# Where a kernel prepares its mixed weight blocks: two of twenty-six moved from the output projection to the up projection, and the weights' high parts taken one chunk earlier in the output projection

## The chip, the cores and the metric

The kernel runs on one core of a Trainium2 chip. The metric is device time in microseconds (us) of one execution; lower is better. Each kernel is run several times and the median counts. One more execution is taken with the hardware profiler; it has a time of its own.

## What is computed

A decoder layer for 256 tokens of width 2048 in float32: RMS norm, one input projection, eight attention heads beside a causal pooling mixer, an output projection into the residual stream, and a gated MLP with a causal convolution of width 3. Cut to what the change touches:

```python
x = x + jnp.concatenate([a, m], axis=-1) @ w_out
h = rms_norm(x, ffn_norm_g)
u = h @ w_up                                  # 2048 -> 2 * 5632
y = conv_b + sum(conv_w[i] * u_pad[:, i:i + S] for i in range(3))
gate, val = jnp.split(y, 2, axis=-1)
x = x + (jax.nn.silu(gate) * val) @ w_down    # 5632 -> 2048
```

## The kernel before

**Chunks.** All weights stream once from HBM in chunks of 128 x 2048 floats (1 MB), in the order of use, numbered c. A chunk feeds two steps of TensorE (PE). The output projection is chunks 32 to 48, the first third of the up projection is chunks 49 to 80. An output-projection block is two chunks (four steps) and yields 256 of the 2048 features; there are eight, 0 to 7. An up-projection group is four chunks: a gate block and a value block. The MLP runs in three thirds of 8, 8 and 6 groups; each third's up projection is followed by its share of the down projection.

**High and low parts.** To get float32 accuracy from float32r matmuls, each raw chunk (`raw`) is split: ACT copies it to a rounded high part (`wh`, line 158 or 181), and VectorE (DVE) subtracts to get the low part (`wl`, line 159 or 187). PE multiplies high by high and low (one 512-column matmul, line 263) and low by high (one 256-column matmul, line 265); these two I call a pair. There are four `wh` buffers, three `wl` buffers and five `raw` buffers (four, and one opened in the output projection); a raw buffer is free again when its low part is made.

**When a chunk is split.** `layer` records the instructions of all engines in one pass over the steps, and each engine executes its own in that order. When chunk c-2 is about to be used, chunk c is handled. Below chunk 52 (`FROM`) both parts of chunk c are recorded there (`split`). From 52 on only the low part of c is (`low`), and the high part of c+1 (`high`), so that ACT is three chunks ahead of PE and DVE two:

```python
            if c < FROM:
                split(c)
            if FROM - 1 <= c < len(rows) - 1:
                high(c + 1)
            if FROM <= c < len(rows):
                splits.append(lambda c=c: low(c))
```

**Mixed blocks.** The down projection saves an eighth of the products of some chunks with sums of weight blocks (Winograd's form of Strassen's seven products). Those sums are made on the chip: `make` loads a 1 MB block (`in_mix`, through the SP queue as all loads), does three DVE operations on it (lines 195, 196, 197), and writes it back to HBM through the POOL queue (`mixed`, line 198); the down projection loads it later like a chunk. The raw buffer of a mix block is free when that write has landed. There are 26 makes. `MAKES` names the chunks of the output projection at which the first ones stand, `PAIRS` the places in each third's up projection, in units of four chunks.

**The end of an output block.** When PE has finished a block, `residual` runs: an ACT copy and a DVE add of the two accumulator halves (`fs`, lines 532 and 533), which frees the accumulator; the DVE add to the residual (`x2f`, line 707); an ACT square and a DVE add into the running sum of squares (`xs`, line 712, and line 713). One step later `x2_split` makes the activations of the next stage (`x2h`, ACT line 721, DVE line 723). After block 7, `sums2` (lines 772 and 745 to 752) reduces the sum of squares, and two small POOL DMAs (`row_d`, `row`, lines 754 and 756) turn it into a row on all partitions, from which `stats2` (lines 384 to 391) makes the norm's factors `rrow`. The first gate block needs them when it leaves its accumulator (line 533 and, times `rrow`, line 788, `u`). Two accumulators exist, so the third up block cannot start before the first has left.

Of the kernel before, what the change touches and what calls it, by code (L numbers as in the profile page):

```python
# [42 lines left out]
CH = 2048  # L43
HALF = CH // 2
AHEAD = 5
FROM = 52
AFTER_DOWN = (97, 145)
RAWS = 4

# [3 lines left out]
WOFF = ((32, 32), (16, 36))  # L53
THIRDS = ((0, 8), (8, 16), (16, 22))
SEVEN = ((1, 2, 3, 4, 5), (1, 2, 3, 4, 5), (1, 2, 3))
MAKES = (40, 42, 44, 46, 48, 50)
PAIRS = ((2, 3, 4, 5, 6, 7), (0, 1, 2, 3, 4, 5, 6, 7), (0, 1, 2, 3, 4, 5))
SOFF, SPAD = 32, 64


# [6 lines left out]
def plan():  # L67

    rows, makes = [(k, i) for i, k in enumerate(24 * ["tok"] + 25 * ["feat"])], list(MAKES)
    n = t = 0  # L70
    for (g0, g1), sevens, pairs in zip(THIRDS, SEVEN, PAIRS):
        makes += [len(rows) + 4 * p + 3 for p in pairs]
        c = rows[-1][1] + 1
        rows += [("feat", c + i) for i in range(4 * (g1 - g0))]
        c = rows[-1][1] + 1
        for i in range(2 * (g1 - g0)):
            if i % (g1 - g0) in sevens:
                rows.append(("sum", t))
                t += 1
            rows.append(("rest" if i % (g1 - g0) in sevens else "tok", c + i))  # L80
    assert len(makes) == t, (len(makes), t)
    return rows, makes
# [12 lines left out]
def layer(ctx: ExitStack, tc: tile.TileContext, xT, wts, mix, par, rel_d, ident_d, icnt_d, out):  # L95
# [24 lines left out]

    raws, wparts = {}, {}
    rows, makes = plan()
    mixed = [dram.tile([P, CH], F32, name=f"mixed{i}", tag=f"mixed{i}") for i in range(len(makes))]
    order = [r for c in range(len(rows)) for r in [c] + [("make", i) for i, m in enumerate(makes) if m == c]]
# [49 lines left out]
    def split(c):  # L174
        split_piece(c, 0, CH)
        release(c)

    def high(c):

        wparts[c] = w, = (high_tile(c)[:, :width(c)],)  # L180
        nc.scalar.activation(w, raws[c][:, :width(c)], AF.Copy)  # L181

    def low(c):

        wh, = wparts[c]
        wl = low_tile(c)[:, :width(c)]
        nc.vector.tensor_tensor(wl, raws[c][:, :width(c)], wh.bitcast(F32), op=OP.subtract)  # L187
        wparts[c] = wh, wl
        release(c)
# [788 lines left out]
    for u in range(n):  # L978
# [4 lines left out]
        elif u in starts:  # L983
            c, now[0] = starts[u] + 2, u
# [6 lines that stand above are left out]
# [91 lines left out]
```

## Time and profile before

| | us |
|---|---|
| median of 3 runs (1008.5 to 1010.6) | 1008.98 |
| the profiled execution's own time | 1016.39 |
| its span, first to last instruction | 1014.6 |
| PE busy | 999.8 |
| PE weight loads busy | 858.5 |
| DVE busy | 846.1 |
| ACT busy | 540.2 |
| POOL busy | 75.0 |
| mean granted TensorE clock | 0.993 |
| moved by DMA | 285.34 MB, 281 GB/s |

The span is the stretch that the profile covers; the own time has a little around it. An engine's busy time is the sum over its instructions, and matmul ends are modelled, so that PE's idle time is better read from the list of its waits. In the trace's rows the first number is the start, the second the duration, both in us; in brackets stands the idle time of the engine before the instruction and what ended it. "L263" is line 263.

### The profile page before, as it was taken

How to read it: one execution, taken by the hardware profiler on the slowest of the kernel's cores; microseconds unless marked ns; L12 is line 12 of the kernel's file. 1: busy time of each engine (PE TensorE's matmuls, PEld its weight loads, DVE VectorE, ACT ScalarE, POOL GpSimd, SP SyncE). 2: the span in 40 equal slices, each digit the busy share in tenths (PEclk: the TensorE clock that was granted, in tenths of full speed). 3: DMA queues.
4: the chain of work that ended last, by engine and by line, in shares of the span. 5: the costliest groups of instructions: out<-in, count | busy, mean ns of one | idle time of the engine just before them, and what ended most of it. 6: DMA issues, size and time to landing. Idle time of an engine off the chain costs nothing.

```text
span 1014.6 us, 13410 instructions
## 1 busy us (share of the span) xinstructions
PE 999.8 (99%) x5276; PEld 858.5 (85%) x5276; DVE 846.1 (83%) x960; ACT 540.2 (53%) x543; POOL 75.0 (7%) x145
## 2 busy tenths in 40 slices
PE   9999999999988999999999999999999999999998
PEld 8888888888877888888888888888888888888886
DVE  6776858858886999899888879999998887899986
ACT  6554545555444554555646455454665745555642
POOL 0202232200002500000000000000000000000000
PEclk9999999999998999999999999999999999999999
DMA  9958785687888987777779777777787977777782
GB/s 348 320 207 271 258 260 177 218 291 290 302 321 284 308 287 283 292 257 289 294 287 379 267 293 278 264 276 278 281 307 314 385 262 301 276 273 277 288 321 85
DMA packets 47679, 285.34 MB, mean 281 GB/s; under 512 B 6568, under 2 KB 9000, under 8 KB 18176
## 3 DMA queue, kind: packets, MB, share of 16 engines
q1 hardware_dynamic: 39184, 245.29, 66.7%
q0 software_dynamic: 8432, 39.20, 10.6%
q8 instruction: 41, 0.67, 0.2%
q14 instruction: 22, 0.18, 0.1%
HBM read 248.94 MB, written 35.52 MB: 280 GB/s over the span
## 4 chain that ended last, share of the span: by engine, by line
PE 71%; DVE 14%; issue 6%; DMA 5%; ACT 2%; POOL 1%; SPq 0%; DVEq 0%; POOLq 0%; ACTq 0%
PE ps_feat L263 29%; PE ps_down L849 21%; PE ps_feat L265 15%; DVE wl L187 5%; PE ps_val L241 4%; PE ps_tok L251 2%; DVE y L800 1%; DVE fs L533 1%; DVE y L798 1%; DMA raw<-in_mix 1%; DVE raw L195 1%; ACT wh L181 1%; DVE u L788 1%; DVE wl L159 1%; DMA qT<-q1d 1%
## 5 line engine op out<-in xcount | busy, mean ns | idle before, releaser
L263 PE MATMUL ps_feat<-x2h,wh 128*128 128x512 f32 x1406 | 490.3, 395 | 5.1 <-DVE x2h L723 3.5
L265 PE MATMUL ps_feat<-x2h,wl 128*128 128x256 f32 x1408 | 392.9, 279 | 2.6 <-DVE wl L187 2.4
L187 DVE TENSOR_TENSOR wl<-raw,wh 128x2048 fp32r<-128x2048 f32 (+1 forms) x155 | 339.2, 2195 | 18.7 <-PE ps_down L849 7.1
L181 ACT ACTIVATE wh<-raw 128x2048 fp32r<-128x2048 f32 (+1 forms) x155 | 285.3, 1844 | 79.0 <-PE ps_down L849 57.2
L263 PEld LDWEIGHTS ps_feat<-x2h,wh 128*128 128x128 f32 x1406 | 266.1, 189 | 65.8 <-DVE x2h L723 3.8
L265 PEld LDWEIGHTS ps_feat<-x2h,wl 128*128 128x128 f32 x1408 | 266.8, 189 | 3.5 <-DVE wl L187 3.0
L159 DVE TENSOR_TENSOR wl<-raw,wh 128x2048 fp32r<-128x2048 f32 (+3 forms) x60 | 119.5, 1999 | 50.0 <-ACT wh L158 38.6
L849 PE MATMUL ps_down<-wh,hid 128*128 128x512 f32 x444 | 142.4, 389 | 0.0
L158 ACT ACTIVATE wh<-raw 128x2048 fp32r<-128x2048 f32 (+3 forms) x60 | 99.9, 1681 | 11.6 <-DMA raw<-in_wts 8.2
L849 PEld LDWEIGHTS ps_down<-wh,hid 128*128 128x128 f32 x444 | 83.3, 188 | 17.3
L263 PE MATMUL ps_feat<-cat,wh 128*128 128x512 f32 x256 | 88.3, 392 | 0.0
L849 PE MATMUL ps_down<-wl,hid 128*128 128x512 f32 x222 | 86.4, 389 | 0.0
L251 PE MATMUL ps_tok<-wh,xh 128*128 128x512 f32 x256 | 80.1, 391 | 0.0
L533 DVE TENSOR_TENSOR fs<-ps_feat,fs 128x512 f32<-128x512 f32 x52 | 35.8, 689 | 49.7 <-ACT fs L532 49.7
L265 PE MATMUL ps_feat<-cat,wl 128*128 128x256 f32 x256 | 71.1, 278 | 0.2 <-DVE wl L159 0.2
L849 PE MATMUL ps_down<-wh,sums 128*128 128x512 f32 x208 | 69.2, 389 | 0.0
L198 POOL DMA_DIRECT2D mixed<-raw x26 | 13.9, 536 | 666.7 <-DVE raw L197 643.2
L263 PEld LDWEIGHTS ps_feat<-cat,wh 128*128 128x128 f32 x256 | 48.0, 188 | 10.4
L251 PEld LDWEIGHTS ps_tok<-wh,xh 128*128 128x128 f32 x256 | 48.1, 188 | 10.0
L824 ACT ACTIVATE hid<-y 128x512 fp32r<-128x512 f32 x22 | 13.9, 633 | 74.7 <-DVE y L823 74.7
L797 ACT ACTIVATE y<-u,pv 128x256 f32<-128x256 f32 x88 | 47.6, 590 | 5.5 <-DVE u L788 5.5
L811 ACT ACTIVATE y<-y 128x512 f32<-128x512 f32 x22 | 13.9, 634 | 68.6 <-DVE y L800 68.6
(186 smaller groups left out, 1100.1 us busy)
## 6 DMA issues: line engine op xcount, KB each, us to landing
raw<-in_wts SPq DMA_DIRECT2D x152, 1024.0 KB, 6.4
raw<-in_mix SPq DMA_DIRECT2D x26, 1024.0 KB, 5.0
mixed<-raw POOLq DMA_DIRECT2D x26, 1024.0 KB, 4.6
raw<-mixed SPq DMA_DIRECT2D x26, 1024.0 KB, 6.2
raw<-in_wts SPq DMA_DIRECT2D x26, 768.0 KB, 5.0
raw<-in_wts SPq DMA_DIRECT2D x4, 512.0 KB, 7.6
x2d<-x2x POOLq DMA_DIRECT2D x4, 512.0 KB, 5.6
x<-x2d POOLq DMA_DIRECT2D x32, 64.0 KB, 4.6
```

The lines of the kernel that those rows point to most:

```text
L158: nc.scalar.activation(wh, w, AF.Copy)
L159: nc.vector.tensor_tensor(wl, w, wh.bitcast(F32), op=OP.subtract)
L181: nc.scalar.activation(w, raws[c][:, :width(c)], AF.Copy)
L187: nc.vector.tensor_tensor(wl, raws[c][:, :width(c)], wh.bitcast(F32), op=OP.subtract)
L198: nc.gpsimd.dma_start(mixed[i], r)
L241: nc.tensor.matmul(ps[b][:, t, :], xh[:, k, a, ts], w[:, ws], start=False, stop=(k == KT - 1 and n == 2), skip_group_check=True)
L251: nc.tensor.matmul(ps[:, t, :], act[:, k0 + k, a, ts], w[:, ws], start=(first and k == 0 and n == 0), stop=(last and k == 1 and n == 2))
L263: nc.tensor.matmul(ps, wh[:, ws], act[:, k, :, :], start=(bool(first) and n == 0), stop=False, skip_group_check=True)
L265: nc.tensor.matmul(ps[:, S:], wl[:, ws], act[:, k, 0, :], start=False, stop=(last and n == len(ks) - 1), skip_group_check=True)
L533: nc.vector.tensor_tensor(dst, ps[:, :, :S], dst, op=OP.add)
L797: nc.scalar.activation(y[:, m, :], u[:, m, 2:], AF.Identity, scale=cw[2], bias=col(C_CB + f))
L849: nc.tensor.matmul(ps, a, w, start=(first and n == 0), stop=(last and n == 2), skip_group_check=True)
```

## The change

Three constants change. Two of the six makes of the output projection (chunks 48 and 50, in blocks 6 and 7) go, and one more stands in the seventh group of the up projection in each of the first two thirds; the number stays 26, and what is computed stays the same. `FROM` falls from 52 to 36, so that chunks 36 to 51 too have their high part made one chunk earlier than their low part.

```diff
-FROM = 52
+FROM = 36
...
-MAKES = (40, 42, 44, 46, 48, 50)
-PAIRS = ((2, 3, 4, 5, 6, 7), (0, 1, 2, 3, 4, 5, 6, 7), (0, 1, 2, 3, 4, 5))
+MAKES = (40, 42, 44, 46)
+PAIRS = ((2, 3, 4, 5, 6, 6.5, 7), (0, 1, 2, 3, 4, 5, 6, 6.5, 7), (0, 1, 2, 3, 4, 5))
...
-        makes += [len(rows) + 4 * p + 3 for p in pairs]
+        makes += [len(rows) + int(4 * p) + 3 for p in pairs]
```

DVE's order in the output projection, from the end of block 5 to the end of block 6, with rows of before marked - and of the change marked + (`x2f` ends a block, `x2h` are the next stage's activations):

```order
 L707 TENSOR_TENSOR x2f<-fs,x2f 128x512
-L159 TENSOR_TENSOR wl<-raw,wh 128x2048
+L187 TENSOR_TENSOR wl<-raw,wh 128x2048
 L723 SCALAR_TENSOR_TENSOR x2h<-x2f,pv,x2h 128x256 x2
-L159 TENSOR_TENSOR wl<-raw,wh 128x2048
-L195 TENSOR_TENSOR raw<-raw 128x1024
-L196 TENSOR_TENSOR raw<-raw 128x512
-L197 TENSOR_TENSOR raw<-raw 128x512
+L187 TENSOR_TENSOR wl<-raw,wh 128x2048
 L533 TENSOR_TENSOR fs<-ps_feat,fs 128x512
 L707 TENSOR_TENSOR x2f<-fs,x2f 128x512
```

The make's three rows are gone; the two low parts stand where they stood, under the line of `low` instead of `split_piece`. The same holds for block 7.

ACT's order at the beginning of the output projection, after the change (`ps_pool` rows belong to the pooling mixer):

```order
L158 ACTIVATE wh<-raw 128x2048 x2
L181 ACTIVATE wh<-raw 128x2048
L563 ACTIVATE cat<-pst 128x2x256
L582 ACTIVATE cat<-ps_pool,pv 128x256 x4
L181 ACTIVATE wh<-raw 128x2048
L582 ACTIVATE cat<-ps_pool,pv 128x256 x4
L181 ACTIVATE wh<-raw 128x2048
L532 ACTIVATE fs<-ps_feat 128x512
```

Before, the row `L181 ACTIVATE wh<-raw 128x2048` above `L563` was not there, and the two further down were high parts of one chunk less: from here on ACT is one chunk further ahead, up to the up projection, where both kernels agree again.

DVE's order in the up projection's seventh group of the second third, after the change (`y` is the convolution, `sums` and `ls` belong to the activations' sums):

```order
L800 SCALAR_TENSOR_TENSOR y<-u_1832,pv,y 128x256
L187 TENSOR_TENSOR wl<-raw,wh 128x2048
L195 TENSOR_TENSOR raw<-raw 128x1024
L196 TENSOR_TENSOR raw<-raw 128x512
L197 TENSOR_TENSOR raw<-raw 128x512
L533 TENSOR_TENSOR fs<-ps_feat,fs 128x512
L788 TENSOR_TENSOR u_1833<-fs,rrow_2608 128x2x256
L187 TENSOR_TENSOR wl<-raw,wh 128x2048
```

Before, `L533` followed directly on the low part `L187`: the added make stands between a low part and the end of the value group's accumulator. The first third has the same added rows at its seventh group.

## The prediction

> **What bounds the kernel now.** I read the list of PE's waits first. PE is busy nearly all of the span, so its few waits must be found one by one.
>
> ```profile
> PE ps_feat L263 <- DVE x2h L723: 3.5, 1, 3.5
> PE ps_feat L265 <- DVE wl L187: 2.4, 1, 2.4
> PE ps_feat L263 <- DVE fs L533: 1.6, 1, 1.6
> ```
>
> The columns are total, times and longest. Each of the three happens once, and PE's timeline puts all of them behind the output projection:
>
> ```profile
> 301.35 0.79 PE L263 MATMUL ps_feat<-x2h,wh 128*128 128x512 f32 x1 [3.47 <-DVE x2h L723]
> 302.15 0.63 PE L263 MATMUL ps_feat<-x2h,wh 128*128 128x512 f32 x1
> 302.79 0.63 PE L263 MATMUL ps_feat<-x2h,wh 128*128 128x512 f32 x1
> ...
> 319.35 0.50 PE L263 MATMUL ps_feat<-x2h,wh 128*128 128x512 f32 x1 [1.65 <-DVE fs L533]
> 322.28 0.58 PE L265 MATMUL ps_feat<-x2h,wl 128*128 128x256 f32 x1 [2.43 <-DVE wl L187]
> ```
>
> The first wait is for the last activations (k = 14, 15) of block 7, the second for the first gate block to leave its accumulator, the third for a low part behind it. After each stall a pair takes 302.79 - 302.15 = 0.64 us. The table by stretches shows why; its last three columns are the granted clock, the DMA share and GB/s:
>
> ```profile
> 300.40:307.30 6.90, 5.95 (x19) 5.09 (x20) 6.78 (x9) 3.68 (x2) 0.64 (x2) 0.51 0.92 379
> 307.30:314.10 6.80, 6.80 (x40) 5.87 (x40) 0.00 (x0) 0.00 (x0) 0.98 (x2) 1.00 0.96 279
> 320.90:327.70 6.80, 5.42 (x17) 4.64 (x18) 6.73 (x8) 5.34 (x6) 3.17 (x6) 0.50 0.77 245
> ```
>
> Two stretches of 6.8 us ran at half clock; the stretch between shows DVE with nothing to do for 6.8 us. A smaller loss starts earlier, at block 6:
>
> ```profile
> 264.08 0.39 PE L263 MATMUL ps_feat<-cat,wh 128*128 128x512 f32 x1
> 264.31 0.28 PE L265 MATMUL ps_feat<-cat,wl 128*128 128x256 f32 x1
> 264.42 0.39 PE L263 MATMUL ps_feat<-cat,wh 128*128 128x512 f32 x1
> ...
> 264.76 0.39 PE L263 MATMUL ps_feat<-cat,wh 128*128 128x512 f32 x1
> 265.13 0.38 PE L265 MATMUL ps_feat<-cat,wl 128*128 128x256 f32 x1
> ...
> 287.98 0.28 PE L265 MATMUL ps_feat<-cat,wl 128*128 128x256 f32 x1
> ...
> 289.23 0.40 PE L263 MATMUL ps_feat<-x2h,wh 128*128 128x512 f32 x1
> ...
> 297.36 0.40 PE L263 MATMUL ps_feat<-x2h,wh 128*128 128x512 f32 x1
> ```
>
> Up to here a pair takes 264.42 - 264.08 = 0.34 us. At 265.13 the low part is about 0.14 us late, and from then on a pair takes 0.354 us (the 23 pairs from 289.23 to 297.36 take 8.13): a slow rhythm that a late low part starts. The row at 287.98 is PE's last of the output projection.
>
> Why DVE is late is in its own timeline (second number the duration):
>
> ```profile
> 270.57 0.68 DVE L533 TENSOR_TENSOR fs<-ps_feat,fs 128x512 f32<-128x512 f32 x1
> 272.74 0.69 DVE L713 TENSOR_TENSOR sq<-sq,xs 128x512 f32<-128x512 f32 x1 [0.76 <-ACT xs L712]
> 274.55 2.29 DVE L159 TENSOR_TENSOR wl<-raw,wh 128x2048 fp32r<-128x2048 f32 x1 [1.11 <-ACT wh L158]
> 279.75 1.22 DVE L195 TENSOR_TENSOR raw<-raw 128x1024 f32<-128x1024 f32 x1
> 282.33 0.68 DVE L533 TENSOR_TENSOR fs<-ps_feat,fs 128x512 f32<-128x512 f32 x1
> 293.04 1.22 DVE L195 TENSOR_TENSOR raw<-raw 128x1024 f32<-128x1024 f32 x1 [1.24 <-DMA raw<-in_mix]
> 295.63 0.68 DVE L533 TENSOR_TENSOR fs<-ps_feat,fs 128x512 f32<-128x512 f32 x1
> 300.83 0.86 DVE L723 SCALAR_TENSOR_TENSOR x2h<-x2f,pv,x2h 128x256 fp32r<-128x256 f32 x2
> 315.20 0.40 DVE L391 TENSOR_SCALAR rs<-row 128x256 f32<-128x256 f32 x1 [7.96 <-DMA row<-row_d]
> 318.61 0.69 DVE L533 TENSOR_TENSOR fs<-ps_feat,fs 128x512 f32<-128x512 f32 x1 [0.72 <-ACT fs L532]
> ```
>
> DVE needs 282.33 - 270.57 = 11.76 us for a block. PE's own pace is the distance of ACT's copies, which start as blocks end:
>
> ```profile
> 243.20 0.60 ACT L532 ACTIVATE fs<-ps_feat 128x512 f32<-128x512 f32 x1 [1.38 <-PE ps_feat L265]
> 254.08 0.60 ACT L532 ACTIVATE fs<-ps_feat 128x512 f32<-128x512 f32 x1 [0.50 <-PE ps_feat L265]
> ```
>
> That is 10.88 us. So DVE, not PE, paces the output projection and falls 0.9 us behind per block; block 7's sum starts at 295.63, 7.6 us after PE's last matmul of the block began. Behind it hangs one chain: squares, `row_d`, `row`, `rrow`, the gate block's exit, the next low part, PE.
>
> **The change part by part.** *High parts three ahead.* Nothing is added: sixteen chunks have the same ACT and DVE instructions in another order. What goes is DVE's wait for ACT before the low part that follows a block's end, in all
>
> ```profile
> DVE wl L159 <- ACT wh L158: 6.7, 6, 1.1
> ```
>
> that is 1.1 us a block. With it a block costs DVE 11.76 - 1.11 = 10.65 us, under PE's 10.88. DVE then gains 0.23 us a block instead of losing 0.88, block 6's low part is no longer late, and the slow rhythm does not start there.
>
> *Two makes gone.* A make is the stretch from L195 to the next L533, 282.33 - 279.75 = 2.58 us; the second one also ended a wait of 1.24 for its mix load. Without them blocks 6 and 7 cost DVE about 8.1 us, so it is waiting for PE at both ends. PE's start of block 6 is 264.76, so block 7 ends at 264.76 + 2 x 10.88 = 286.5, and block 7's sum on DVE starts some 0.6 later (ACT's copy lasts 0.60), at 287.1 instead of 295.63: 8.5 us earlier. The last activations end at 287.1 + (300.83 + 0.86 - 295.63) = 293.2. PE wants them three and a quarter steps into the up projection (10.88 / 4 = 2.72 a step): 286.5 + 8.8 = 295.3. The first wait is gone, with 2 us to spare, and so is its half-clock stretch. PE reaches the third up block at 264.76 + 4 x 10.88 = 308.3; before it was there at 319.35 - 1.65 = 317.7.
>
> *What is late next.* The chain through the two small DMAs. It took 315.20 - 295.63 = 19.6 us from block 7's sum to L391, and 322.28 - 315.20 = 7.1 from there to PE's restart, both untouched by the change. Moved by 8.5 it restarts PE at 313.8, 5.5 us after PE got there. The transit can shrink, since it ran beside the last make's write:
>
> ```profile
> SPq L150 <- DMA mixed<-raw: 61.8, 6, 12.3
> ...
> DMA to landing us min/median/max: 4.6/9.7/11.4
> ...
> DMA to landing us min/median/max: 8.0/8.0/8.0
> ...
> DMA to landing us min/median/max: 5.7/5.7/5.7
> ```
>
> (SP's own waits from 225 to 310 us; then the landing times of the six makes' writes there, of `row` and of `row_d`.) The upper bound is today's 5.7 + 8.0. For the lower, both land like the fastest write, 2 x 4.6: 4.5 us less. Loads still stream, so I take a third of that, 1.5 us. PE restarts at 312.3 (308.3 and no wait at the one end, 313.8 at the other): 322.28 - 312.3 = **10.0 us** gained, bounds 8.5 and 14.0.
>
> *Clock.* Before, both half-clock stretches cost; the first one's loss is already in PE's arrival time. The second lasts 327.7 - 322.28 = 5.4 us after the restart, half of it lost: 2.7. Today's two waits add up to 4.1, tomorrow's to 4.0 with a matmul between, so I take the same loss again: 0 (bounds 2.7 gained, 0.7 lost if a whole stretch of 6.8 falls behind the restart). The Trainium skill, "TensorE: Matmul & The Clock Gate", section "HAM oscillation — how this bites in real kernels", puts the danger at idle gaps above about 3.4 us. The first wait here agrees; the other two, 1.65 and 2.43, are each shorter and the clock dropped all the same. By that rule no stretch would follow, and the total would be 2.7 lower.
>
> *One more make in the seventh group of two thirds.* Here DVE was late already in the second third:
>
> ```profile
> 713.47 2.28 DVE L187 TENSOR_TENSOR wl<-raw,wh 128x2048 fp32r<-128x2048 f32 x1
> 721.17 0.69 DVE L533 TENSOR_TENSOR fs<-ps_feat,fs 128x512 f32<-128x512 f32 x1 [0.78 <-ACT fs L532]
> 740.67 0.69 DVE L533 TENSOR_TENSOR fs<-ps_feat,fs 128x512 f32<-128x512 f32 x1 [0.36 <-ACT fs L532]
> ...
> 748.57 0.50 PE L849 MATMUL ps_down<-wl,sums 128*128 128x512 f32 x1 [0.45 <-DVE wl L187]
> ```
>
> From the make's place, just ahead of 721.17, to PE's wait at 748.57 DVE idles only 0.78 + 0.36. So 2.58 - 1.14 = 1.4 us come out as PE's wait at the least. Two mix loads and two writes now fall in one group, as dense as in the output projection, where writes landed in 9.7 us, so ACT's loads may come late too. I take a whole make, **2.6 us lost**; ends 0 and, if both thirds pay in full, 5.2. In the first third PE runs the slow rhythm, whose group lasts 0.9 us longer; that slack is the cover, and without it the first third costs its 2.6 as well. POOL and SP queues: the moved writes and loads stand behind weight loads only; nobody waits for a mixed block before the down projection.
>
> *Sum.* -10.0 + 2.6 = -7.4 us against the profiled execution's 1016.39. That one is 7.4 us above the median of the runs, for reasons it does not show; its waits come from DVE's order, which is the same in every run, so I take the difference over as it is: 1008.98 - 7.4 = **1001.6 us**.
>
> **The rivals.** *The row chain keeps most of it* (1005). ACT now asks for each raw chunk one chunk (5.4 us) earlier, in front of the block's own copy. A load that is late holds `fs`, and block 7's sum with it. SP's 61.8 us of waits for writes speak for it, the four buffered loads against. If block 7's sum moves 5 instead of 8.5, the gain is 6.5 - 2.6 = 4.
>
> *Clock stays full after the shorter wait* (1001.6 - 2.7 = 999): for it the rule above, against it that 1.65 and 2.43 did not save it.
>
> *The first third runs in the fast rhythm* (996). Were PE to wait so little that no low part is late, its remaining 448 pairs would each save 0.014: 6.3 us, of which DVE, then without its slack, gives back some 1. Against it: the late low part at 265.13 left the rhythm slow through the next three blocks, and one stands behind the row chain again.
>
> *Slower* (1011). The same starved ACT, but worse. The place is the load of chunk 48, which waits for the third make's write. If that write and the loads behind it come more than 8.5 us later than ACT wants them, block 7's sum stands where it does today, and what is left is the added makes' 2.6. SP's longest wait for a write was 12.3 us, 1.4 more than a block, so three blocks would bring arrears of some 4 us; it decides only at twice that.
>
> *No change* (1009): the sum moves just enough to pay for the added makes.
>
> **How the numbers follow.** Forecast 1001.6 with 0.47; row chain 0.17; full clock 0.12; fast rhythm 0.11; no change 0.05; slower 0.08. About 0.2%, 2 us, is what a measurement can tell from no change. Faster by more is 0.47 + 0.17 + 0.12 + 0.11 = 0.87, same 0.05, slower 0.08. The range goes down to 995, the fast rhythm with most of its price, and up to 1007, a row chain that keeps all but 2 us; no change and slower lie outside, with the last of the fast rhythm less than 0.2.
>
> **What would show it.** Right: no wait on L723; block 7's L533 within 2 us of PE's last pair of the output projection; one half-clock stretch behind the row; a wait of 2 to 6 us on L533 and L187 at the third up block; PE's wait near the start of the second third's down projection up by 1 to 3 us. Wrong: high parts (L181) waiting for raw loads in blocks 5 to 7, or a first wait that stays.

## The result, and the profile after

The changed kernel takes 999.9 us (median of 4 runs, 997.5 to 1001.8) against 1009.8 for the kernel before (4 runs, 1008.5 to 1011.8) on the same chip: ratio 0.990, 95% interval 0.987 to 0.993. A second set gave 998.4 (996.7 to 998.7), ratio 0.987 (0.985 to 0.990). The forecast was 1001.6 us and faster than before. So the time came out; four of the terms behind it did not, and the agreement is in part luck, as the section on the prediction shows.

The profiled execution of the changed kernel took 1001.79 us (span 1000.0). The list of PE's waits has lost all three that the prediction began with:

```profile
PE ps_down L849 <- DVE wl L187: 5.6, 6, 2.9
...
PE ps_feat L265 <- DVE wl L187: 0.5, 1, 0.5
```

The half us lies late, at 438.4; nothing waits behind the output projection. The table by stages (length, PE busy, and so on to the granted clock, DMA share and GB/s) shows what this did. First before, then after; the rows are the first third's up projection, its down projection, and the second third's down projection:

```profile
288.10:482.90 194.80, 187.08 (x1026) 160.50 (x1025) 166.34 (x208) 100.12 (x106) 24.42 (x45) 0.96 0.81 292
482.90:563.20 80.30, 80.30 (x357) 66.49 (x356) 70.41 (x51) 48.99 (x32) 0.00 (x0) 1.00 0.82 315
...
737.50:818.50 81.00, 80.55 (x356) 66.37 (x355) 72.95 (x54) 50.75 (x34) 0.00 (x0) 1.00 0.87 333
```

```profile
285.20:460.10 174.90, 174.39 (x1027) 154.38 (x1025) 158.50 (x200) 94.93 (x102) 24.43 (x45) 1.00 0.80 290
460.10:542.80 82.70, 80.79 (x356) 66.33 (x355) 74.49 (x57) 50.55 (x34) 0.00 (x0) 1.00 0.84 334
...
717.20:803.90 86.70, 83.04 (x355) 67.35 (x355) 75.16 (x57) 53.62 (x37) 0.00 (x0) 0.98 0.89 342
```

The up projection of the first third is 19.9 us shorter, the two down projections are 2.4 and 5.7 longer. With 1.5 in the output projection, 1.4 ahead of it (where nothing was changed) and 0.1 given back in the second third, the spans differ by 14.6. The medians differ by only 9.9, because the execution profiled before, 1016.4 us, was longer than any of 73 later runs of that kernel, which lie between 1005.8 and 1016.3; the one profiled after was the longest of its four, by less.

DVE's timeline shows why no wait is left (the rows answer to those at 295.63, 300.83, 315.20 and 318.61 before):

```profile
286.01 0.69 DVE L533 TENSOR_TENSOR fs<-ps_feat,fs 128x512 f32<-128x512 f32 x1 [0.58 <-ACT fs L532]
291.22 0.86 DVE L723 SCALAR_TENSOR_TENSOR x2h<-x2f,pv,x2h 128x256 fp32r<-128x256 f32 x2
298.39 0.40 DVE L391 TENSOR_SCALAR rs<-row 128x256 f32<-128x256 f32 x1 [0.75 <-DMA row<-row_d]
301.80 0.69 DVE L533 TENSOR_TENSOR fs<-ps_feat,fs 128x512 f32<-128x512 f32 x1 [0.72 <-ACT fs L532]
303.13 2.29 DVE L187 TENSOR_TENSOR wl<-raw,wh 128x2048 fp32r<-128x2048 f32 x1
```

From block 7's sum to L391 it is 298.39 - 286.01 = 12.4 us, before 19.6. The two small transfers now land in

```profile
row<-row_d POOLq DMA_DIRECT2D x1, 128.0 KB, 4.9
row_d<-qrow POOLq DMA_DIRECT2D x1, 1.0 KB, 1.6
```

(last column, us), before 8.0 and 5.7. The loads beside them had paused: while `row_d` landed, the DMA engines were 0.05 busy and moved 15 GB/s, where before they were 1.00 busy and moved 421 (last two columns, after and before):

```profile
291.50:293.20 1.70, 1.70 (x11) 1.51 (x10) 1.70 (x3) 1.13 (x1) 0.52 (x1) 1.00 0.05 15
```

```profile
301.20:306.90 5.70, 5.55 (x17) 4.78 (x18) 5.70 (x5) 2.88 (x2) 0.50 (x1) 0.50 1.00 421
```

PE reaches the third up block at 285.2 + 4 x 5.44 = 307.0, and its low part is ready at 303.13 + 2.29 = 305.4, 1.5 us ahead. No stall, so the clock stays full (before, 0.51 in this stretch), and PE's pairs stay in the quick rhythm, here 420.50 - 420.16 = 0.34 us:

```profile
300.40:307.30 6.90, 6.90 (x43) 6.14 (x42) 6.04 (x10) 4.68 (x6) 1.82 (x4) 1.00 0.61 223
```

```profile
420.16 0.39 PE L263 MATMUL ps_feat<-x2h,wh 128*128 128x512 f32 x1
420.38 0.28 PE L265 MATMUL ps_feat<-x2h,wl 128*128 128x256 f32 x1
420.50 0.39 PE L263 MATMUL ps_feat<-x2h,wh 128*128 128x512 f32 x1
```

So the 19.9 us are about: 7.55 - 0.51 = 7.0 of waits; 2.97 + 2.71 = 5.7 of half clock (half of PE's busy 5.95 and 5.42 us in the two stretches); and, for some 490 pairs at 0.014 us, 6.9 of rhythm. Together 19.6.

What came back is in the second third's down projection. On ACT, DVE and PE in turn:

```profile
717.07 1.92 ACT L181 ACTIVATE wh<-raw 128x2048 fp32r<-128x2048 f32 x1 [4.71 <-DMA raw<-mixed]
```

```profile
719.51 0.48 DVE L798 SCALAR_TENSOR_TENSOR y<-u,pv,y 128x256 f32<-128x256 f32 x1 [1.84 <-ACT y L797]
```

```profile
732.33 0.50 PE L849 MATMUL ps_down<-wl,sums 128*128 128x512 f32 x1 [2.86 <-DVE wl L187]
```

```profile
733.40:736.80 3.40, 3.40 (x10) 2.68 (x9) 3.40 (x3) 2.00 (x3) 0.00 (x0) 0.51 0.99 308
```

DVE, one make later than before, also waits 1.84 us for ACT, which waited for a mixed block to come from memory; PE's wait of 2.86 us is followed by 3.4 us at half clock.

### The profile page after: what moved, and what is told of

It reads as the page before. It is cut to its first block, busy times and chain, and to the rows that moved or that the text cites. A ratio compares the mean times of both kernels' runs of the same rounds, so it can differ in the third digit from the quotient of the medians.

```text
span 1000.0 us, 13401 instructions
## 1 busy us (share of the span) xinstructions
PE 987.8 (99%) x5276; PEld 852.7 (85%) x5276; DVE 846.0 (85%) x960; ACT 540.4 (54%) x543; POOL 74.7 (7%) x145
## 4 chain that ended last, share of the span: by engine, by line
PE 80%; DVE 8%; DMA 5%; issue 4%; ACT 1%; POOL 1%; SPq 0%; POOLq 0%; DVEq 0%; ACTq 0%
PE ps_feat L263 35%; PE ps_down L849 20%; PE ps_feat L265 18%; PE ps_val L241 4%; DVE wl L187 3%; PE ps_tok L251 2%; DMA raw<-mixed 1%; DVE y L800 1%; DMA qT<-q1d 1%; DVE y L798 1%; DMA eT<-e3d 1%; DMA q0d<-q0x 1%; ACT wh L181 1%; DMA eT<-e0d 1%; PE ps_pool L272 1%
## 5 line engine op out<-in xcount | busy, mean ns | idle before, releaser
L263 PE MATMUL ps_feat<-x2h,wh 128*128 128x512 f32 x1406 | 478.4, 389 | 0.0
L187 DVE TENSOR_TENSOR wl<-raw,wh 128x2048 fp32r<-128x2048 f32 (+1 forms) x171 | 375.6, 2204 | 21.8 <-issue 7.0
L265 PE MATMUL ps_feat<-x2h,wl 128*128 128x256 f32 x1408 | 388.9, 276 | 0.5 <-DVE wl L187 0.5
L181 ACT ACTIVATE wh<-raw 128x2048 fp32r<-128x2048 f32 (+1 forms) x171 | 315.8, 1851 | 104.3 <-PE ps_down L849 61.0
L159 DVE TENSOR_TENSOR wl<-raw,wh 128x2048 fp32r<-128x2048 f32 (+3 forms) x44 | 83.0, 1895 | 38.3 <-ACT wh L158 29.0
L533 DVE TENSOR_TENSOR fs<-ps_feat,fs 128x512 f32<-128x512 f32 x52 | 35.9, 690 | 51.1 <-ACT fs L532 51.0
L158 ACT ACTIVATE wh<-raw 128x2048 fp32r<-128x2048 f32 (+3 forms) x44 | 69.3, 1598 | 11.1 <-DMA raw<-in_wts 6.5
L849 PEld LDWEIGHTS ps_down<-wl,hid 128*128 128x128 f32 x222 | 42.0, 189 | 10.4 <-DVE wl L187 1.8
```

Source lines behind the costliest of these rows:

```text
L158: nc.scalar.activation(wh, w, AF.Copy)
L159: nc.vector.tensor_tensor(wl, w, wh.bitcast(F32), op=OP.subtract)
L263: nc.tensor.matmul(ps, wh[:, ws], act[:, k, :, :], start=(bool(first) and n == 0), stop=False, skip_group_check=True)
L265: nc.tensor.matmul(ps[:, S:], wl[:, ws], act[:, k, 0, :], start=False, stop=(last and n == len(ks) - 1), skip_group_check=True)
L533: nc.vector.tensor_tensor(dst, ps[:, :, :S], dst, op=OP.add)
L849: nc.tensor.matmul(ps, a, w, start=(first and n == 0), stop=(last and n == 2), skip_group_check=True)
```

## The experiments

All medians in us, with their ranges and the ratio to the kernel before, run beside them (its medians there 1009.8 to 1011.4); the last three columns are stages of the profiled execution, first third up, first third down, second third down. A profile is one execution: with the high parts alone, the two empty transfers, the split matmul and the makes in the down projection it was the shortest of the runs, 3.6, 2.5, 3.2 and 1.3 us under the median, so there these columns lie on the low side. Diffs are against the changed kernel, where nothing else is said.

| kernel | median (range) | ratio [95%] | up 1 | down 1 | down 2 |
|---|---|---|---|---|---|
| before | | | 194.8 | 80.3 | 81.0 |
| changed, first / second set | 999.9 / 998.4 | 0.990 / 0.987 | 174.9 / 176.1 | 82.7 / 81.9 | 86.7 / 82.8 |
| makes alone | 1003.6 (1002.6-1004.8) | 0.992 [0.989, 0.995] | 181.5 | 80.3 | 81.9 |
| high parts alone | 1008.1 (1004.5-1012.4) | 0.997 [0.994, 0.999] | 185.5 | 80.3 | 81.0 |
| two empty transfers | 1011.8 (1009.3-1014.0) | 1.000 [0.998, 1.003] | 187.7 | 82.0 | 81.9 |
| two empty loads | 1004.4 (1003.2-1006.2) | 0.994 [0.992, 0.996] | 181.4 | 82.7 | 82.0 |
| before, split matmul | 1014.0 (1010.8-1016.5) | 1.003 [1.001, 1.005] | 190.1 | 80.3 | 80.2 |
| row chain 3.7 later | 1001.3 (1000.6-1002.4) | 0.991 [0.988, 0.993] | 177.8 | 82.8 | 82.9 |
| no added makes | 995.4 (994.0-996.1) | 0.985 [0.981, 0.988] | 175.1 | 81.1 | 80.3 |
| six makes early | 1001.9 (1001.2-1006.4) | 0.992 [0.989, 0.995] | 176.9 | 80.3 | 81.1 |
| five makes | 1000.3 (998.0-1004.9) | 0.990 [0.986, 0.993] | 181.4 | 80.2 | 80.3 |
| make in second group | 1002.2 (1001.2-1003.1) | 0.991 [0.989, 0.994] | 182.0 | 82.0 | 80.3 |
| makes in down projection | 1004.2 (1003.0-1010.8) | 0.995 [0.994, 0.997] | 174.8 | 85.5 | 84.9 |

**The change in two halves.** The makes alone, with the high parts as before:

```diff
-FROM = 36
+FROM = 52
```

> Only the two makes are moved; high parts stay two chunks ahead as before. Theory 1 (two causes: DVE is no longer behind at block 7, and the row's two small transfers meet emptier queues; together they spare PE every stall behind the output projection): DVE still loses 0.9 us a block up to block 5, so block 6's low part is as late as before and the slow rhythm starts there and stays to the end of the first third (some 7 us of pairs at 0.354 instead of 0.340), but the sum of block 7 comes near 289 us and the row near 301, so there is no stall at the third up block. 1003 to 1006 us. Theory 2 (the moved makes are the whole gain): the same as the changed kernel, 1000 us.

The high parts alone, with the makes as before:

```diff
-MAKES = (40, 42, 44, 46)
-PAIRS = ((2, 3, 4, 5, 6, 6.5, 7), (0, 1, 2, 3, 4, 5, 6, 6.5, 7), ...
+MAKES = (40, 42, 44, 46, 48, 50)
+PAIRS = ((2, 3, 4, 5, 6, 7), (0, 1, 2, 3, 4, 5, 6, 7), ...
```

> Only FROM = 36; the six makes stay in the output projection, none is added in the up projection. Theory 1: DVE keeps up with PE, the quick rhythm lasts through the output projection, but the last two makes' loads and writes are in the queues when the row is sent (transit 18 to 20 us from block 7's sum to L391 instead of 12.4), PE waits 4 to 7 us at the third up block, drops to half clock once and runs the first third slowly; the two down projections do not lose what the added makes cost (8 us in the changed kernel's profile). 1000 to 1004 us. Theory 2: no gain, 1009 us.

Makes alone win 0.8%, high parts alone 0.3%; that is 1.1% together, against 1.0 and 1.3% for the whole change. Each figure is uncertain by 0.2 to 0.3%, and within that they add up. The lists of PE's waits, makes alone first, say what each leaves:

```profile
PE ps_down L849 <- DVE wl L187: 1.4, 1, 1.4
PE ps_feat L265 <- DVE wl L187: 1.2, 1, 1.2
```

```profile
PE ps_feat L263 <- DVE fs L533: 3.0, 1, 3.0
PE ps_feat L265 <- DVE wl L187: 2.4, 1, 2.4
PE ps_feat L263 <- DVE x2h L723: 1.6, 1, 1.6
```

With the high parts alone all three old waits remain. The makes end the stalls; the high parts add 1.5 us in the output projection (92.9 us with them alone and in the whole change, 94.0 with the makes alone, 94.4 before). With the makes alone one wait of 1.2 us is left at the third up block, and from there to its end the first third runs in the slow rhythm.

Neither theory 1 held in full. With the makes alone the slow rhythm was to start at block 6. There the low part was as late as before (one pair of 264.35 - 263.75 = 0.60 us, before 265.35 - 264.76 = 0.59), block 7's was even 0.6 us late, and PE stayed quick until the third up block. With the high parts alone 1000 to 1004 us were expected, and a slow first third behind the stalls; it took 1008.1, and in its profile the pairs were quick again after the half-clock stretch (400.33 - 399.99 = 0.34 us). So stalls and half clock do not by themselves bring the slow rhythm.

**Is it DVE's work or the queue's?** Two extra mix loads and writes stood at chunks 48 and 50 of the changed kernel, with no DVE work between them:

```diff
+order = [x for r in order for x in [r] + [("ghost", i) for m, i in {48: 0, 50: 1}.items() if m == r]]
...
+nc.gpsimd.dma_start(spare[GHOST[c]], raws.pop(("ghost", GHOST[c]))), later(2, load_next)
```

> The changed kernel, with two more mix blocks loaded and written to a spare place at chunks 48 and 50, as the kernel before did, but with no DVE work on them: the queues of before with the DVE order of the change. Theory 1: the row's transit goes back to 18 to 20 us, PE stalls 4 to 7 us at the third up block, half clock and slow rhythm follow: 1006 to 1012 us. Theory 2 (DVE's 2.6 us per make is all that counted): within 2 us of the changed kernel.

The whole gain went, with none of DVE's 2 x 2.58 us back (the added makes stay, so this kernel carries two transfers each way more than the kernel before). PE's longest wait was for block 7's activations, 5.1 us; at the third up block, where I had expected 4 to 7, it waited 0.7 and 2.4. DVE, ACT and the queue's own waits (SP, 225 to 310 us):

```profile
293.10 0.69 DVE L533 TENSOR_TENSOR fs<-ps_feat,fs 128x512 f32<-128x512 f32 x1 [4.20 <-ACT fs L532]
```

```profile
290.67 1.92 ACT L181 ACTIVATE wh<-raw 128x2048 fp32r<-128x2048 f32 x1 [4.49 <-DMA raw<-in_wts]
292.49 0.57 ACT L532 ACTIVATE fs<-ps_feat 128x512 f32<-128x512 f32 x1
```

```profile
SPq L150 <- DMA spare<-raw: 16.1, 2, 9.8
```

```profile
row<-row_d POOLq DMA_DIRECT2D x1, 128.0 KB, 6.4
row_d<-qrow POOLq DMA_DIRECT2D x1, 1.0 KB, 4.6
```

SP holds its next load until the write has freed a buffer, ACT's high part waits for that load, and the block's copy `fs` stands behind it: block 7's sum comes at 293.10, 7.1 us later than in the changed kernel. The small transfers take 4.5 us longer. The same without the writes (the buffers are freed at once; against the kernel with the transfers):

```diff
-(nc.gpsimd.dma_start(spare[GHOST[c]], raws.pop(("ghost", GHOST[c]))), later(2, load_next))
+(raws.pop(("ghost", GHOST[c])), later(2, load_next))
```

> The changed kernel with two extra 1 MB loads at chunks 48 and 50 whose data nobody uses, and no write: the kernel with two empty transfers without its two writes. Theory A (the writes do it: SP holds its next load until the write has landed, and the small transfers of row stand beside a write): the third up block waits little or not, time 999.9-1003. Rival (two more loads crowd the rest as much as the writes): waits as there, time 1005-1010.

1004.4, between the two: block 7's sum is only 1.5 us late (287.53), while `row_d` and `row` still take 4.2 and 7.1, and PE waits 1.6 and 2.4 us at the third up block, against theory A. Loads alone slow the small transfers; the writes hold the blocks.

**The added makes.** Without them:

```diff
-... for i, m in enumerate(makes) if m == c]]
+... for i, m in enumerate(makes) if m == c and i not in (9, 18)]]
-src, n = mixed[i] if kind == "sum" else wts[i], n or width(c)
+src, n = (mix[i] if i in (9, 18) else mixed[i]) if kind == "sum" else wts[i], n or width(c)
```

> The changed kernel without the two makes that were put into the seventh groups of the first and second third: their two blocks of the down projection are read from the unmixed input instead, so two of the 26 mixes are left out (VectorE's work, the write to memory and its wait; the load stays). Theory A (the added makes cost what the two down projections grew by, 2.4 and 5.7 us): first down projection 80-81, second 80-82, time 991-994. The prediction's term (2.6 us for both): 997. Rival (they cost nothing, the second down projection grew for another reason): 999-1001.

995.4 us, 1.4 above theory A, and 3.0 to 4.5 less than the changed kernel's two medians (which did not run beside it), from the down projections (81.1 and 80.3). The forecast had 2.6, with ends 0 and 5.2. The 2.4 and 5.7 of the first profile are the larger of two: in the second set the stages grew by 1.6 and 1.8, PE's longest wait was 1.7 us, and the clock did not drop.

**The rhythm.** If it is a late low part that slows PE's pairs, then it should do so in the changed kernel as well. VectorE's first transpose behind the row was done four times:

```diff
-        nc.vector.transpose(...)
+        for _ in range(4 if q == 0 else 1): nc.vector.transpose(...)
```

> The changed kernel, with VectorE's first transpose behind the output projection (line 731, 1.23 us) done four times in place of once: 3.7 us more on VectorE, so that the third up block's low part should land some 1 to 2 us behind TensorE's need instead of 1.5 us ahead of it. Theory A (one late low part there sets TensorE's pairs from 0.340 to 0.354 us for the rest of the first third): the first third's up projection goes from 174.9 to 180-183 us, the first down projection from 82.7 back to 80-81, the time to 1003-1006. Rival (a wait costs its own length and nothing more): the up projection 176-177, the time 1001-1002.

My theory fell. The wait came, as long as the one in the kernel with the makes alone, and after four pairs at 0.35 us the rhythm was quick again (350.28 - 349.94 = 0.34 us):

```profile
308.54 0.39 PE L265 MATMUL ps_feat<-x2h,wl 128*128 128x256 f32 x1 [1.12 <-DVE wl L187]
...
349.94 0.39 PE L263 MATMUL ps_feat<-x2h,wh 128*128 128x512 f32 x1
350.17 0.28 PE L265 MATMUL ps_feat<-x2h,wl 128*128 128x256 f32 x1
350.28 0.39 PE L263 MATMUL ps_feat<-x2h,wh 128*128 128x512 f32 x1
```

The kernel with five makes showed the reverse:

```diff
-MAKES = (40, 42, 44, 46)
-PAIRS = (..., (0, 1, 2, 3, 4, 5, 6, 6.5, 7), ...)
+MAKES = (38, 40, 42, 44, 46)
+PAIRS = (..., (0, 1, 2, 3, 4, 5, 6, 7), ...)
```

> The changed kernel with five makes at chunks 38, 40, 42, 44, 46, and without the added one in the second third (the first third keeps its seven). Theory A (each make costs by its place; the second third's added one cost 6.4 us of the profiles, one more in the output projection stands where VectorE has slack): second down projection 80-81.5 in place of 86.7, first down projection and output projection within 1.5 us of the changed kernel, time 994-997. Rival (any fifth make in the output projection brings the loads of its last blocks late, as six did): output projection 95-99 in place of 92.9, time 1000-1003.

Its second down projection fell to 80.3 as theory A had it, and the output projection took 93.9. But the total did not move, for a reason that neither theory had:

```profile
263.24 0.39 PE L263 MATMUL ps_feat<-cat,wh 128*128 128x512 f32 x1
263.48 0.38 PE L265 MATMUL ps_feat<-cat,wl 128*128 128x256 f32 x1
263.70 0.39 PE L263 MATMUL ps_feat<-cat,wh 128*128 128x512 f32 x1
...
275.51 0.40 PE L263 MATMUL ps_feat<-cat,wh 128*128 128x512 f32 x1
275.74 0.28 PE L265 MATMUL ps_feat<-cat,wl 128*128 128x256 f32 x1
275.86 0.40 PE L263 MATMUL ps_feat<-cat,wh 128*128 128x512 f32 x1
```

```profile
286.10:467.50 181.40, 181.22 (x1027) 156.28 (x1026) 161.79 (x204) 96.09 (x104) 24.50 (x45) 1.00 0.82 290
```

One low part at 263.48 was some 0.1 us late (a pair of 0.46 in place of 0.34), and PE ran at 0.35 a pair to the end of the first third: 181.4 us, PE never waiting more than 0.2, against 174.9 in the changed kernel, which waited 0.5. So the rhythm alone is worth 6.5 to 7 us here, and it can start without a wait that the list shows. In the kernel before (the diff is against it), one more accumulator, at chunk 57, had its first matmul split in two, to break the rhythm up:

```diff
-AFTER_DOWN = (97, 145)
+AFTER_DOWN = (57, 97, 145)
```

> The kernel before, with the first matmul of the third group's gate block (chunk 57) split into two of 256 columns, as it already is behind a down projection, where the quick rhythm follows. Theory 1: the slow rhythm of the first third (194.8 us there against 174.9 in the changed kernel, of which 12 us are rhythm, clock and stalls) is a state of the pairs that a late low part starts and the split ends: the remaining 14 blocks save up to 6.3 us, of which DVE's lag takes back 1 to 3: 1003 to 1006 us, and pairs at 0.340 after chunk 57. Rival: the rhythm follows the load on memory in the first third, and the split changes nothing: 1009 us, pairs at 0.354.

It did not help (1014.0 us, 0.3% slower), and the trace shows the slow rhythm starting at the split (L260) itself, in a stretch that had been quick since 322:

```profile
341.20 0.39 PE L263 MATMUL ps_feat<-x2h,wh 128*128 128x512 f32 x1
341.42 0.28 PE L265 MATMUL ps_feat<-x2h,wl 128*128 128x256 f32 x1
341.54 0.39 PE L260 MATMUL ps_feat<-x2h,wh 128*128 128x256 f32 x2
...
342.97 0.40 PE L263 MATMUL ps_feat<-x2h,wh 128*128 128x512 f32 x1
343.21 0.28 PE L265 MATMUL ps_feat<-x2h,wl 128*128 128x256 f32 x1
343.33 0.40 PE L263 MATMUL ps_feat<-x2h,wh 128*128 128x512 f32 x1
```

An irregular pair can thus tip PE into the slow spacing, or leave it alone. Even the same event went both ways. Block 6's low part came about 0.14 us late in the kernel before, with the makes alone and in this kernel; only the first turned slow there. Block 7's came 0.6 us late in the other two, and only this kernel turned slow. And an irregular pair can end the slow spacing: without the added makes the pairs were slow from 417 until a low part came 0.1 us late at 439.70, and quick behind it. What decides is open.

**Other places for the two makes.** At the start of the output projection, six in all:

```diff
+MAKES = (36, 38, 40, 42, 44, 46)
+PAIRS = ((2, 3, 4, 5, 6, 7), (0, 1, 2, 3, 4, 5, 6, 7), ...
```

> The changed kernel with six makes at chunks 36, 38, 40, 42, 44, 46 and no added ones: the two go to the start of the output projection, where VectorE was busy 6.55 of 12 us between 204 and 216, instead of the seventh groups. Theory A (a make costs by where it stands: VectorE's slack and no write behind block 4): output projection still 92.5-93.5 us, both down projections 80-82, time 991-995. Rival 1 (the first writes hold SP's queue and the loads come late, so that blocks 5 to 7 wait as in the kernel with the two empty transfers): output projection and row late, a wait at the third up block, time 1000-1006. Rival 2 (the added makes were not what the down projections paid for): 999-1001.

The down projections were short (80.3 and 81.1), but the output projection took 98.8 us. ACT's row says why; the block's copy stood behind it and PE then waited 3.3 us at 278.64:

```profile
271.08 1.92 ACT L181 ACTIVATE wh<-raw 128x2048 fp32r<-128x2048 f32 x1 [7.31 <-DMA raw<-in_wts]
```

It is rival 1's cause, one block earlier. In the second group of the first third, which had no make:

```diff
+PAIRS = ((1, 2, 3, 4, 5, 6, 6.5, 7), (0, 1, 2, 3, 4, 5, 6, 7), ...
```

> The changed kernel with the second third's added make moved to the first third's second group, which had none: eight makes in each of these thirds, four in the output projection. Theory A (VectorE needs 20.1 us for a group without a make and 22.7 with one, TensorE 21.8): the second down projection falls to 80-81.5, the first third pays one make, 2.6 us, in its last groups and its down projection, time 996-999. Rival (the make lands on the row chain's heels and TensorE waits again at the third and later up blocks, with the slow rhythm): the first third's up projection 180 and more, time 1001-1006.

The rival was right: eight makes put DVE behind, PE waited four times on a low part, 4.9 us in all from 352 on, and slow stretches followed. Last, inside the down projections:

```diff
+PAIRS = ((2, 3, 4, 5, 6, 7, 8.25), (0, 1, 2, 3, 4, 5, 6, 7, 8.25), ...
```

> The changed kernel with its two added makes four chunks into the down projections of the first and second third in place of the seventh groups: the up projections then have one make a group at most, the last sum that needs each is read late enough. Theory A (VectorE was busy 72.3 to 72.8 us of a down projection of 80 to 81 without the added make, so that 2.6 more fit; the queue carried 336 GB/s and takes two transfers more): down projections 80-82, time 994-997. Rival (the down projection's transfers are already dense, 0.87 of the engines' time, and a write and a mix load bring its raw loads late): down projections 84-90, time 1000-1010.

Again the rival, 85.5 and 84.9 us. ACT waited for mixed blocks, 5.9 us at once, in the first of them:

```profile
ACT wh L181 <- DMA raw<-mixed: 7.3, 2, 5.9
```

None of the four places beats the changed kernel.

## Why the prediction was right, and where it was not

- *High parts three ahead.* Right in the main. From 225 to 290 us DVE waits for no high part any more, and block 6's low part is not late. But blocks 5 and 6 did not keep up: their sums came 2 us late (the row of block 6 stands first below), because ACT's copy stood behind a high part. In block 6 that high part had waited for its load, the row-chain rival's mechanism and my sign against. PE did not wait for it, and block 7's copy was again PE's to release:

```profile
277.37 0.69 DVE L533 TENSOR_TENSOR fs<-ps_feat,fs 128x512 f32<-128x512 f32 x1 [2.02 <-ACT fs L532]
```

```profile
269.90 1.93 ACT L181 ACTIVATE wh<-raw 128x2048 fp32r<-128x2048 f32 x1 [1.68 <-DMA raw<-in_wts]
...
274.93 1.92 ACT L181 ACTIVATE wh<-raw 128x2048 fp32r<-128x2048 f32 x1 [2.31 <-DMA raw<-in_wts]
...
285.38 0.60 ACT L532 ACTIVATE fs<-ps_feat 128x512 f32<-128x512 f32 x1 [1.44 <-PE ps_feat L265]
```

- *Two makes gone.* Block 7's sum at 286.0, forecast 287.1, and the first wait is gone. The reason was half right: I put it all on DVE's 2.58 us each. The empty transfers show that the same traffic holds that sum back by 7.1 us with no DVE work.
- *What is late next: the row chain.* This step failed. I let it shrink by 1.5 us, 4.5 at most, from its 13.7 us of transit, since loads still stream; it shrank by 13.7 - 6.5 = 7.2. The loads did not stream: the DMA engines were 0.05 busy when `row_d` went. And the bound was wrong because I took the fastest write, 1 MB in 4.6 us, as the least for a transfer of 1 KB; that one took 1.6. So PE, forecast to restart at 312.3, passed the third up block without a stop at 307.0.
- *Clock.* Forecast 0, and a half-clock stretch behind the row. There was none: with no stall nothing set it off. Of the 5.7 us of half clock in the profiles the forecast already had the first stretch's 3.0 in PE's arrival time; the other 2.7 were one of its bounds.
- *The rhythm.* I gave the quick first third 0.11, because a late low part would stand behind the row chain again. None stood there, and 6.5 to 7 us were won in the profiles. My rule behind it, that a late low part starts the slow rhythm, is too strong, as the kernels with the later row chain and with the makes alone show. The late low part of block 6, on which it rested, was there in the makes-alone kernel too and started nothing.
- *The added makes.* 2.6 forecast, 3.0 to 4.5 in the medians, 8.1 in the first profile and 3.4 in the second. That the first third pays once it has lost its slack was written down and not put in the sum: quick, its group of four chunks takes PE 21.8 us and DVE, with a make, 22.7 (its rows L533 at 389.25 and 411.98 are one group apart).
- *The sum.* -7.4 against -9.9 in the medians. In the profiles it was -21.4 for the output projection and the first third's up projection, where I had -10.0, and +8.1 where I had +2.6. That I carried a difference from a long profiled execution over to the medians hid part of the first error, and that is luck. I had assumed that this kernel's stalls come alike each time; they do not. The kernel with the split matmul is the same up to 341 us, and in its profile the first wait was 1.94 us instead of 3.47, with no half clock behind it, and the small transfers took 4.7 and 6.8 us instead of 5.7 and 8.0. Each kernel was profiled once or twice, so how often each rhythm comes is not shown.

## What to carry to other kernels

A piece of work that is moved takes its transfers along: price the load, the write, and what a queue holds behind the write, before the engine time. When a stall goes, ask which states may go with it: in the profiles half clock and a slow matmul spacing were worth 12.6 us, the stalls themselves 7.0. Half clock went with the stalls; the spacing turned at irregular pairs, and whether it goes is not sure. The engine with slack in a slow stretch may have none once the stretch is quick.

## What was not expected of the hardware

- The same two small transfers, 1 KB out and 128 KB back in, took 1.6 + 4.9 us with the DMA engines 0.05 busy as the first one landed (1.6 and 4.2 to 5.2 in seven of the profiles), 3.0 + 6.2 at 0.27, 4.2 + 7.1 at 0.68, and 5.7 + 8.0 at 1.00, before. The 4.2 + 7.1 had no 1 MB write beside them, so loads are enough.
- A train of 512- and 256-column matmuls has two spacings at full clock, 0.340 and 0.354 us a pair. It turned slow after a low part 0.1 us late, after a wait of 1.2 us, and at a split matmul with no wait at all; it did not after another wait of 1.1 us, and a low part equally late (0.14 or 0.6 us) turned it in one kernel and not in another.
- A single wait of 2.86 us was followed by half clock (0.51 for 3.4 us), and so was one of 3.31 us in the kernel with six makes; single waits of up to 2.2 us were not. The Trainium skill, "TensorE: Matmul & The Clock Gate", section "HAM oscillation — how this bites in real kernels", sets the danger above about 3.4 us of idling; the measurement puts it lower here.
